# The prompt trunk's neighbourhood attention: all 32 probability tiles turned through VectorE and DRAM, value strips copied in the second head group only

## The chip, the cores and the metric

The kernel runs on one core of one Trainium2 chip. The metric is the device time of one execution in microseconds (us). Before the change it is 2136.32 us, the median of three runs (2136.04 to 2136.45).

Five engines work side by side, each through its own queue of instructions in order: TensorE (PE, matmuls; its weight loads are listed as PEld), VectorE (DVE), ScalarE (ACT), GpSimd (POOL) and SyncE (SP). SP issues most transfers (DMAs), ACT and POOL some. An instruction that waits holds back all that stands behind it in its queue. A "q" behind an engine's name in the profile (SPq, ACTq) is that queue, where DMAs are issued.

## What is computed

One layer of an encoder over two sequences, `x_sample` (512 tokens) and `x_prompt` (1024 tokens). The part that matters here, shortened:

```python
z = xn @ w_in                       # q,k,v of branch A, q,k,v of branch B, two gates
o_a = _gqa_attention(qa, ka, va)    # full attention, 8 heads of 64
o_b = _neighbourhood_attention(qb, kb, vb, rpb)
merged = sigmoid(ga) * (o_a @ w_proj_a) + sigmoid(gb) * (o_b @ w_proj_b)
h = x + merged @ w_out
y = h + relu(rmsnorm(h) @ w_mlp_up) ** 2 @ w_mlp_down
```

In branch B each block of 128 queries (two rows of 64 tokens) sees a band of rows of keys, masked to a window of 16 columns, with a learned bias: `p = softmax(q k^T * scale + bias)`, then `p v`. `p` has queries on the partitions, while its product with v needs keys there: each probability tile has to be transposed.

## The kernel before

All products of float32 values are made in three matmuls of halves: each operand is split into a high part (a rounded copy, made by ACT) and a low part (the remainder, a subtraction by DVE). Line 212 issues all these matmuls; lines 199 and 206 are ACT's and DVE's halves of the splits of weights. A weight tile so passes from DRAM by SP (`raw_...`, line 245), through ACT (high) and DVE (low), to PE.

The two sequences are worked off in turn: first the sample (`NB == 1`), then the prompt (`NB == 2`, about 440 to 1100 us), then the MLP of both. The change touches the prompt only, "the long branch". Its stages:

1. **Two groups of heads (g = 0, 1), each with projections and attention A.** The projections of q, k and v take x (`xs`) against split weights; `zs` and `zvs` are their results in PSUM, `zvs` that of v of branch B (weights `raw_vs`, split into `wh_vs` and `wl_vs`). v of branch B is stored to DRAM (`vds`) for use by row bands. Rope tables (`rts`, line 708) come by SP. Then attention A: scores and exponentials (`ps`), transposes of the probabilities on PE (line 823) with ACT and DVE splitting them (828, 829), outputs `os` (791, 792), `ot_As` and `os_As`, stored to DRAM by ACT (`oads`, line 435). Gate matmuls `gpss` are dealt between them as filling work (`fill.pull`), their results stored as `zgs`.
2. **Value strips.** Branch B wants v in four sets of columns. In attention A of both groups, two copies a unit go from DRAM to DRAM (`vsts<-vds`, lines 801 to 811), each with the four heads of its group: 16 copies of 256 KB a group, on SP. A semaphore of eight, shared by SP's and ACT's DMAs in rotation, makes a copy wait for an earlier DMA, among these ACT's stores of attention.
3. **Branch B: 32 units**, eight heads by four query blocks in the order j = 1, 2, 0, 3 (names end in head and j: `_6_2`). A loop over i runs the steps of several units at once: scores of unit i (`s_unit`: `sbs` on PE, `sbss` on DVE, exponential `pbs` on ACT, scaling by POOL), the transposed and split tile of an earlier one (`t_unit`: `bhs`), the product with v of one before that (`v_unit`: `obs` on PE, `ot_Bs` and `os_Bs` behind it). In each round `f` steps of filling work are pulled, at first projections of the next heads (`pqbs`, `pkbs`, weights `w_bqs`, `w_bks`) and the gates, from i = 25 on projection A (`ppas`, one step is three matmuls of 512 columns, results added by DVE to `mAs`).
4. **Projection B (`ppbs`), the output projection,** and later the MLP.

A tile is transposed in one of two ways. The first 24 units (the set `moved`) take the detour: `turn` (line 1094) transposes 32x32 blocks in place on DVE (STREAM_TRANSPOSE) and stores the tile to DRAM (`tbs`, line 1097); `fetch_t` reads it back with the blocks moved (`bhs<-tbs`, line 1104); ACT makes the high part (line 1116, 128x768), DVE the low one (1117); `v_unit` uses six matmuls of 256 columns. The turn comes one round behind the scores, the fetch two, the split three and the output four. The last eight units (heads 6 and 7) are transposed on PE: six matmuls into two PSUM tiles (`ptbs`, line 1126), two ACT copies (1133) and two DVE subtractions (1134) of 128x384, one round behind the scores, and `v_unit` one more behind with four matmuls (two of 512 columns, two of 256).

The order of each engine's instructions is not simply that of the code. A scheduler orders them as the program is built, by its own estimates, except where the code keeps the program's order. PSUM has four buffers for `ppas`, `gpss`, `obs` and `ptbs` together and two for scores.

Of the kernel before, what the change touches and what calls it, by code (L numbers as in the profile page):

```python
# [22 lines left out]
GRID_W = 64  # L23
# [38 lines left out]
def encoder(ctx: ExitStack, tc: tile.TileContext, xs, outs, w):  # L62
# [356 lines left out]
    def run(tr, nxt, first):  # L419
# [109 lines left out]
        for g in range(2):  # L529
# [230 lines left out]
            with phase(f"phA{N}_{g}") as ph:  # L760
                units = [(h, qb) for h in range(4) for qb in range(NB)]
                PP = {}

                def s_tile(u, j):
                    h, qb = u
                    nm = f"{N}_{g}_{h}_{qb}_{j}"
                    q0 = (qb * 4 + j) * P
                    lhs = qT[h % 2][:, h // 2, q0 : q0 + P]
                    s = big(f"s{nm}")[:, :T]
                    for kb in range(NB):  # L770
                        ks = slice(kb * 512, kb * 512 + 512)
                        nc.tensor.matmul(s[:, ks], lhs, kT[:, 0, ks], start=True, stop=False)
                        nc.tensor.matmul(s[:, ks], lhs, kT[:, 1, ks], start=False, stop=True)  # L773
                    nm_ = sml.tile([P, 1], F32, tag="nm", name=f"nm{nm}")
                    nc.vector.tensor_reduce(nm_, s, axis=AX.X, op=ALU.max, negate=True)  # L775
                    p = ph.tile([P, T], F32, tag="P", name=f"p{nm}", bufs=8)
                    l = sml.tile([P, 1], F32, tag="l", name=f"l{nm}")
                    nc.scalar.activation(p, s, AF.Exp, bias=nm_, accum_out=l)  # L778
                    rl = sml.tile([P, 1], F32, tag="rl", name=f"rl{nm}")
                    nc.vector.reciprocal(rl, l)  # L780
                    nc.gpsimd.tensor_scalar(p, p, rl, 1.0, op0=ALU.mult, op1=ALU.mult)  # L781
                    PP[u, j] = p

                o_of = {}

                def pv(u, kc, hi, lo):
                    h, qb = u
                    if kc == 0:
                        o_of[u] = mm(f"o{N}_{g}_{h}_{qb}")
                    o = o_of[u]  # L790
                    nc.tensor.matmul(o, vhl[:, kc, :], hi, start=(kc == 0), stop=False)
                    nc.tensor.matmul(o, vhl[:, kc, :], lo, start=False, stop=(kc == NT - 1))
                    if kc == NT - 1:
                        r0 = (g * 4 + h) * HD
                        finish_o(o, 512, oad[r0 : r0 + HD, qb * 512 : qb * 512 + 512], ph, f"A{N}_{g}_{h}_{qb}")

                for j in range(4):
                    s_tile(units[0], j)
                    fill.pull(2)
                queue = []  # L800
                LAG = 2
                for ui, u in enumerate(units):
                    h, qb = u
                    if NB == 2:
                        hs = slice(4 * g, 4 * g + 4)
                        for a in range(2 * (ui % 2), 2 * (ui % 2) + 2):
                            c0 = (0, 8, 24, 32)[ui // 2]
                            nc.sync.dma_start(
                                vst[ui // 2][:, :, a, hs, :].rearrange("k c h d -> k c (h d)"),
                                vd[:, hs, :].rearrange("(k a c) h d -> a k c (h d)", a=4, c=GRID_W)[a, :, c0 : c0 + 32],  # L810
                            )
                    if first:
                        bias_row(g * 4 + ui)
                        if g == 0 and ui == 1:
                            early["a"] = load_a(1)
                        if g == 0 and ui == 2:
                            early["v"] = load_v(1, slot)
                    nxt_u = units[ui + 1] if ui + 1 < len(units) else None
                    sdone = 0
                    for kc in range(NT):  # L820
                        pt = mm(f"pT{N}_{g}_{h}_{qb}_{kc}")
                        for j in range(4):
                            nc.tensor.transpose(  # L823
                                pt[:, j * P : (j + 1) * P], PP[u, j][:, kc * P : (kc + 1) * P], ident
                            )
                        hi = ph.tile([P, 512], F32R, tag="pth", name=f"pth{N}_{g}_{h}_{qb}_{kc}", bufs=3)
                        lo = ph.tile([P, 512], F32R, tag="ptl", name=f"ptl{N}_{g}_{h}_{qb}_{kc}", bufs=3)
                        nc.scalar.activation(hi, pt, AF.Copy)  # L828
                        nc.vector.tensor_tensor(lo, pt, hi.bitcast(F32), op=ALU.subtract)  # L829
                        queue.append((u, kc, hi, lo))  # L830
                        if nxt_u is not None:
                            while sdone < 4 and kc >= ((0, 1, 3, 4) if NB == 2 else (0, 0, 1, 2))[sdone]:
                                s_tile(nxt_u, sdone)
                                sdone += 1

                        fill.pull(1 if NB == 1 or kc % 4 < 3 else 0)
                        if len(queue) > LAG:
                            pv(*queue.pop(0))
                fill.drain()
                for item in queue:  # L840
                    pv(*item)
# [80 lines left out]
        with phase(f"phB{N}") as ph:  # L922
# [2 lines left out]
            rects, strips, bms, PT = {}, {}, {}, {}  # L925
            units = [(h, j) for h in range(8) for j in (1, 2, 0, 3)]
            n = len(units)
            moved = set(units[: n - 8]) if NB == 2 else set()

            def raw_here(name):  # L930
                if NB == 2:
# [157 lines left out]
            def turn(u):  # L1089

                h, j = u
                pm = PT[u]
                blocks = pm.rearrange("p b f k i -> p (b f k) i")
                tc.keep_in_program_order(nc.vector.transpose(blocks, blocks))
                PT[u] = dram.tile([P, 4, halves * nkc * 32], F32, name=f"tb{N}_{h}_{j}")
                with behind("SP"):
                    nc.sync.dma_start(PT[u], pm.rearrange("p b f k i -> p b (f k i)"))

            def fetch_t(u):

                h, j = u
                hl = ph.tile([P, 2, 4, halves, nkc, 32], F32R, tag="bh", name=f"bh{N}_{h}_{j}", bufs=3)
                with behind("SP"):
                    op = nc.sync.dma_start(
                        hl[:, 1].rearrange("p a f k i -> p a (f k i)").bitcast(F32),
                        PT[u].rearrange("(a i) b w -> (i b) a w", i=32),
                    )
                note("SP", op)
                PT[u] = hl
# [77 lines left out]
            for i, u in enumerate(units):  # L1187
                ls = 3 if u in moved else 3 - NB
                due_t.setdefault(i + ls, []).append(u)
                due_v.setdefault(i + ls + 1, []).append(u)  # L1190
            for i in range(n + 4 - NB):
                if moved:
                    slot_no[0] = i
                if i < n - 8:
                    f = (5 if i < 2 else 2 + i % 2) if NB == 1 else 5 - (i % 6 == 5)
                else:
                    f = 3 + i % 2 if NB == 1 else 8
                if NB == 2 and i == n - 11:
                    pa = proj_a(ph, raw_here)
                    next(pa)  # L1200
                if i < n:
                    late = i > 0 and units[i - 1] in moved
                    if i > 1 and units[i - 2] in moved:
                        fetch_t(units[i - 2])
                    s_unit(units[i], partial(turn, units[i - 1]) if late else None)
                    h, j = units[i]
                    if j == 1 and h < 7:
                        if moved:
                            prep_bias(h + 1)
                        else:  # L1210
                            prep(h + 1)
                    if moved and h > 0:
                        with behind("SP"):
                            prep_v(h, j)
                    if i % 8 == 6 and i + 2 < n:

                        qp = qkproj(i // 8 + 1, wqk, qk)
                        for _ in range(NC8):
                            next(qp)
                    if i % 8 == 7 and qp is not None:  # L1220
                        for _ in qp:
                            pass
                        qp = None
                        if i + 1 < n - 8:
                            wqk = load_qk(i // 8 + 2, held)
                if NB == 2 and i == n - 7:
                    for u in due_v.pop(i):
                        v_unit(u)
                    fill.drain()
                    fill.add(pa)  # L1230
                fill.pull(f // 2)
# [745 lines left out]
```

## Time and profile before

| | |
|---|---|
| median of three runs | 2136.32 us |
| the profiled execution's own time | 2136.87 us |
| its span, first to last instruction | 2135.0 us |
| mean granted clock of PE | 0.997 |
| PE busy | 2099.9 us |
| attention A of group 0, of group 1 | about 452 to 587, 650 to 785 us |
| branch B's units | about 782 to 1059 us |
| projection A in it | 998 to 1059 us |

A row of a stretch ("windows") gives its start and end, its length, then the busy time of PE, PEld, DVE, ACT and POOL with their instructions, the granted clock, the DMA engines' share and GB/s. A row of a timeline gives start, duration, engine, line, operation, out<-in, and in brackets the idle time before it with its releaser. "x6" in it stands for six instructions that follow each other; a duration of one matmul holds some fill time that overlaps with the next, so the step from start to start is the price. A row of waits gives the total, how often, and the longest.

### The profile page before, as it was taken

The page shows a single profiled execution, that of the slowest core. Times are in us where ns is not written, and L with a number is a line of the kernel's source. Part 1 is how long each engine was busy: PE and PEld are TensorE (multiplying, and loading weights), DVE is VectorE, ACT ScalarE, POOL GpSimd, SP SyncE. Part 2 cuts the span into 40 slices and gives each one's busy share as a digit, 9 for nine tenths or more (in the row PEclk, how much of TensorE's full clock was granted, in tenths as well). Part 3 has the DMA queues.
Part 4 walks back from the last instruction along what each step waited for, and adds up shares of the span by engine and source line. Part 5 has one row for each costly group of instructions (what it writes and reads, how often), then busy time and mean ns, then how long its engine had stood idle before and what let it go on. Part 6 is the DMA issues. An engine that isn't in the chain of part 4 may idle for free.

```text
span 2135.0 us, 31762 instructions
## 1 busy us (share of the span) xinstructions
PE 2099.9 (98%) x10871; PEld 1840.2 (86%) x10871; DVE 1483.2 (69%) x2793; ACT 1146.3 (54%) x2487; POOL 362.0 (17%) x446
## 2 busy tenths in 40 slices
PE   9999999999989999999999999999999999999998
PEld 8888778988888888888888899999999988888887
DVE  6665786767647756787882877778777777759563
ACT  6664653767556645555531556556655643434352
POOL 2232310323233314442101200003000000000000
PEclk9999999999999999999999999999999999999999
DMA  6437557520133038876472666578445799688561
GB/s 192 133 99 212 148 165 254 184 89 29 59 111 107 25 97 245 244 219 196 153 246 103 203 196 193 162 249 210 158 146 158 259 351 344 215 276 282 166 203 64
DMA packets 340072, 381.31 MB, mean 179 GB/s; under 512 B 30911, under 2 KB 267079, under 8 KB 339911
## 3 DMA queue, kind: packets, MB, share of 16 engines
q1 hardware_dynamic: 301687, 313.99, 46.9%
q10 hardware_dynamic: 31072, 45.11, 6.0%
q0 software_dynamic: 7152, 20.19, 3.5%
q8 instruction: 86, 1.41, 0.3%
q14 instruction: 75, 0.61, 0.1%
HBM read 282.68 MB, written 105.71 MB: 182 GB/s over the span
## 4 chain that ended last, share of the span: by engine, by line
PE 53%; DVE 1%; issue 0%; ACT 0%; POOLq 0%; POOL 0%; ACTq 0%; DVEq 0%
PE dn L212 20%; PE ua L212 6%; PE ud L212 6%; PE uc L212 6%; PE ops L212 4%; PE ub L212 3%; PE ppbs L212 2%; PE ppas L212 2%; PE dnf L212 2%; PE pt L353 0%; PE obs L212 0%; PE gpss L212 0%; PE sbs L212 0%; PE ptbs L1126 0%; DVE A L1452 0%
## 5 line engine op out<-in xcount | busy, mean ns | idle before, releaser
L212 PE MATMUL dn<-wd,ah 128*128 128x512 f32 x1248 | 384.3, 389 | 0.0
L212 PEld LDWEIGHTS dn<-wd,ah 128*128 128x128 f32 x1248 | 234.2, 188 | 48.7
L212 PE MATMUL dn<-wd,al 128*128 128x512 f32 x624 | 242.8, 389 | 0.0
L1451 ACT ACTIVATE ah<-ar 128x512 fp32r<-128x512 f32 x168 | 104.4, 628 | 206.0 <-PE dn L212 186.7
L212 PE MATMUL gpss<-xs_0h,w_gs 128*128 128x512 f32 x512 | 188.7, 402 | 0.8 <-DVE ot_Bs L472 0.4
L1452 DVE TENSOR_TENSOR al<-ar,ah 128x512 fp32r<-128x512 f32 x168 | 114.4, 687 | 75.5 <-ACT ah L1451 67.9
L212 PE MATMUL ud<-B,A 128*128 128x384 f32 x768 | 143.6, 334 | 0.7 <-DVE c L1569 0.7
L212 PE MATMUL uc<-B,A 128*128 128x384 f32 x768 | 143.7, 334 | 0.0
L212 PE MATMUL ua<-B,A 128*128 128x384 f32 x768 | 138.8, 334 | 0.0
L212 PEld LDWEIGHTS dn<-wd,al 128*128 128x128 f32 x624 | 117.1, 188 | 24.2
L781 POOL TENSOR_SCALAR ps<-ps,rls 128x1024 f32<-128x1024 f32 (+1 forms) x96 | 96.8, 1010 | 226.4 <-DVE rls L780 201.0
L212 PEld LDWEIGHTS ud<-B,A 128*128 128x128 f32 x768 | 133.9, 188 | 1.1 <-DVE c L1569 1.1
L212 PEld LDWEIGHTS uc<-B,A 128*128 128x128 f32 x768 | 134.1, 188 | 0.2 <-ACT A L1451 0.2
L212 PEld LDWEIGHTS ua<-B,A 128*128 128x128 f32 x768 | 133.7, 188 | 0.2
L829 DVE TENSOR_TENSOR ptls<-pTs,pths 128x512 fp32r<-128x512 f32 x160 | 107.7, 686 | 37.3 <-ACT pths L828 36.3
L828 ACT ACTIVATE pths<-pTs 128x512 fp32r<-128x512 f32 x160 | 94.0, 597 | 73.4 <-PE pTs L823 71.3
L212 PE MATMUL ops<-wh_os,mgs 128*128 128x512 f32 x384 | 119.4, 390 | 0.0
L775 DVE TENSOR_REDUCE nms<-ss 128x1 f32<-128x1024 f32 (+1 forms) x96 | 99.9, 1041 | 25.6 <-PE ss L773 25.1
L212 PEld LDWEIGHTS gpss<-xs_0h,w_gs 128*128 128x128 f32 x512 | 96.3, 189 | 18.9 <-DVE w_gs L206 0.7
L778 ACT ACTIVATE ps<-ss,nms 128x1024 f32<-128x1024 f32 (+1 forms) x96 | 93.2, 972 | 23.4 <-DVE nms L775 20.6
L180 POOL TENSOR_TENSOR rs_f<-ms_f,mhalf 128x1 f32<-128x1 f32 x6 | 4.0, 667 | 590.7 <-DVE ms_f L176 590.7
L823 PEld LDWEIGHTS pTs<-ident,ps 128*128 128x128 f32 x640 | 77.7, 140 | 28.6 <-POOL ps L781 4.3
(287 smaller groups left out, 5152.4 us busy)
## 6 DMA issues: line engine op xcount, KB each, us to landing
ar<-ud SPq DMA_DIRECT2D x120, 512.0 KB
br<-in_w_mlp_down_dram SPq DMA_DIRECT2D x72, 512.0 KB
rawu<-in_w_mlp_up_dram SPq DMA_DIRECT2D x64, 512.0 KB
ud<-c ACTq DMA_DIRECT2D x128, 192.0 KB
raw_gs<-in_w_in_dram SPq DMA_DIRECT2D x32, 512.0 KB
ud<-cs SPq DMA_DIRECT2D x64, 192.0 KB
tbs<-pbs SPq DMA_DIRECT2D x24, 384.0 KB
bhs<-tbs SPq DMA_DIRECT2D x24, 384.0 KB
```

What stands on the lines that cost most here:

```text
L180: nc.gpsimd.tensor_tensor(r[:, :n], m[:, :n], mhalf[:, :n], op=ALU.pow)
L212: op = nc.tensor.matmul(out, a, b, **kw)
L775: nc.vector.tensor_reduce(nm_, s, axis=AX.X, op=ALU.max, negate=True)
L778: nc.scalar.activation(p, s, AF.Exp, bias=nm_, accum_out=l)
L781: nc.gpsimd.tensor_scalar(p, p, rl, 1.0, op0=ALU.mult, op1=ALU.mult)
L823: nc.tensor.transpose(pt[:, j * P : (j + 1) * P], PP[u, j][:, kc * P : (kc + 1) * P], ident)
L828: nc.scalar.activation(hi, pt, AF.Copy)
L829: nc.vector.tensor_tensor(lo, pt, hi.bitcast(F32), op=ALU.subtract)
L1451: nc.scalar.activation(hi, src, AF.Copy)
L1452: nc.vector.tensor_tensor(lo, src, hi.bitcast(F32), op=ALU.subtract)
```

## The change

Three edits, all for the prompt:

- The strip copies are made in group 1 only, and each takes all eight heads: 16 copies of 512 KB instead of 32 of 256 KB.
- `moved` holds all 32 units. The last eight take the detour too, with its lags of three and four rounds, so the loop has two rounds more (i to 35). `fetch_t` and the last `turn` get conditions of their own, since there are no more scores beside them, and a `v_unit` that came early at i = 25 is no longer taken out.
- From i = 24 on six steps of filling work are pulled a round instead of eight.

```diff
@@ attention A
-                    if NB == 2:
-                        hs = slice(4 * g, 4 * g + 4)
+                    if NB == 2 and g == 1:
                         for a in range(2 * (ui % 2), 2 * (ui % 2) + 2):
                             c0 = (0, 8, 24, 32)[ui // 2]
                             nc.sync.dma_start(
-                                vst[ui // 2][:, :, a, hs, :].rearrange("k c h d -> k c (h d)"),
-                                vd[:, hs, :].rearrange("(k a c) h d -> a k c (h d)", a=4, c=GRID_W)[a, :, c0 : c0 + 32],
+                                vst[ui // 2][:, :, a].rearrange("k c h d -> k c (h d)"),
+                                vd.rearrange("(k a c) h d -> a k c (h d)", a=4, c=GRID_W)[a, :, c0 : c0 + 32],
                             )
@@ branch B
-            moved = set(units[: n - 8]) if NB == 2 else set()
+            moved = set(units) if NB == 2 else set()
...
-            for i in range(n + 4 - NB):
+            for i in range(n + 3 if NB == 1 else n + 4):
...
-                    f = 3 + i % 2 if NB == 1 else 8
+                    f = 3 + i % 2 if NB == 1 else 6
...
+                if 1 < i < n + 2 and units[i - 2] in moved:
+                    fetch_t(units[i - 2])
+                if i == n and moved:
+                    turn(units[i - 1])
                 if i < n:
                     late = i > 0 and units[i - 1] in moved
-                    if i > 1 and units[i - 2] in moved:
-                        fetch_t(units[i - 2])
                     s_unit(units[i], partial(turn, units[i - 1]) if late else None)
...
                 if NB == 2 and i == n - 7:
-                    for u in due_v.pop(i):
-                        v_unit(u)
                     fill.drain()
```

How the order moves is seen in three places. Lines behind the first edit are one lower in the kernel after.

First, SP at the end of group 0 and the start of group 1 (`rawkvs` and `raw_vs` are weights of the k and v projections, `rts` rope tables). Before:

```order
L510 DMA rawkvs_1_7022<-in_w_in_dram 128x8x64 x2
L808 DMA vsts_0_4661<-vds_4660 128x1x512 x4
L808 DMA vsts_1_4662<-vds_4660 128x1x512 x4
L808 DMA vsts_2_4663<-vds_4660 128x1x512 x4
L808 DMA vsts_3_4664<-vds_4660 128x1x512 x4
L245 DMA raw_vs_1_0_7031<-in_w_in_dram 128x4x256
L245 DMA raw_vs_1_4_7038<-in_w_in_dram 128x4x256
L708 DMA rts_1_0_7047<-in_rope_dram 128x128
```

After:

```order
L510 DMA rawkvs_1_7006<-in_w_in_dram 128x8x64 x2
L245 DMA raw_vs_1_0_7015<-in_w_in_dram 128x4x256
L245 DMA raw_vs_1_4_7022<-in_w_in_dram 128x4x256
L245 DMA raw_gs_2304_4_0_7603<-in_w_in_dram 128x8x128
L708 DMA rts_1_0_7031<-in_rope_dram 128x128
```

The sixteen copies of group 0 are gone from between the weights of k and those of v.

Second, ACT at the end of attention A and the start of branch B (`qBs` and `kBs` are the first heads' q and k out of `pqbs` and `pkbs`). Before:

```order
L435 DMA zgs_0_4665<-sgs_2304_7_1_9215 128x512
L475 ACTIVATE ot_As_1_3_1_9222<-os_1_3_1_9142 64x512
L435 DMA oads_4667<-os_As_1_3_1_9224 64x512
L992 ACTIVATE qBs_0_9258<-pqbs_0_0_9261 64x4x128 x2
L1013 ACTIVATE kBs_0_0_9259<-pkbs_0_0_9296 64x512 x2
```

After:

```order
L435 DMA zgs_0_4665<-sgs_2304_7_1_9199 128x512
L475 ACTIVATE ot_As_1_3_1_9206<-os_1_3_1_9126 64x512
L435 DMA oads_4667<-os_As_1_3_1_9208 64x512
L199 ACTIVATE w_bqs_0_9226<-raw_bqs_0_0_9224 128x1024
L199 ACTIVATE w_bks_0_9232<-raw_bks_0_0_9230 128x1024
L199 ACTIVATE w_gs_3328_0_9238<-raw_gs_3328_0_0_9236 128x1024
L991 ACTIVATE qBs_0_9242<-pqbs_0_0_9245 64x4x128 x2
```

Before, the split of `w_bqs_0` stands some 115 rows earlier, among attention's exponentials; after, three splits stand behind attention's last store and ahead of `qBs`.

Third, PE in projection A. Before, from one output to the next:

```order
L212 MATMUL obs_6_2_11752<-bhs_6_2_11608,vss_6_11406 128x512 x2
L212 MATMUL obs_6_2_11752<-bhs_6_2_11608,vss_6_11406 128x2x128 x2
L212 MATMUL sbs_7_1_11765<-kBs_3_1_11132,qBs_3_11130 128x384 x4
L212 MATMUL ppas_3_0_11799<-oXs_0_0_11033,w_pas_3_11691 128x512 x3
L212 MATMUL ppas_3_0_11799<-oXs_0_1_11036,w_pas_3_11691 128x512 x3
L212 MATMUL ppas_3_0_11799<-oXs_0_2_11037,w_pas_3_11691 128x512 x3
L212 MATMUL ppas_3_0_11799<-oXs_0_3_11038,w_pas_3_11691 128x512 x3
L1126 MATMUL ptbs_6_3_0_11815<-ident,pbs_6_3_11677 128x128 x3
L1126 MATMUL ptbs_6_3_1_11816<-ident,pbs_6_3_11677 128x128 x3
L212 MATMUL ppas_3_1_11828<-oXs_0_0_11033,w_pas_3_11691 128x512 x3
```

(three more steps of `ppas` follow.) After:

```order
L212 MATMUL obs_6_2_11812<-bhs_6_2_11599,vss_6_11390 128x2x128 x6
L212 MATMUL sbs_7_0_11828<-kBs_3_1_11116,qBs_3_11114 128x384 x4
L212 MATMUL ppas_3_1_11803<-oXs_0_2_11021,w_pas_3_11651 128x512 x3
L212 MATMUL ppas_3_1_11803<-oXs_0_3_11022,w_pas_3_11651 128x512 x3
L212 MATMUL ppas_4_0_11872<-oXs_0_0_11017,w_pas_4_11781 128x512 x3
L212 MATMUL ppas_4_0_11872<-oXs_0_1_11020,w_pas_4_11781 128x512 x3
L212 MATMUL ppas_4_0_11872<-oXs_0_2_11021,w_pas_4_11781 128x512 x3
L212 MATMUL ppas_4_0_11872<-oXs_0_3_11022,w_pas_4_11781 128x512 x3
L212 MATMUL obs_6_0_11890<-bhs_6_0_11677,vss_6_11390 128x2x128 x6
```

The transposes `ptbs` are gone, an output is six matmuls, a round has six steps of `ppas`, and the outputs come two rounds later against the scores.

## The prediction

> **What bounds the kernel now.** I read the page's busy line first, then the waits of TensorE (PE) alone over the prompt trunk (440 to 1070 us), since only that trunk is touched.
>
> ```profile
> PE 2099.9 (98%) x10871; PEld 1840.2 (86%) x10871; DVE 1483.2 (69%) x2793; ACT 1146.3 (54%) x2487; POOL 362.0 (17%) x446
> PE zvs L212 <- ACT wh_vs L199: 5.7, 1, 5.7
> PE sbs L212 <- DVE kBs L1015: 2.3, 2, 1.8
> PE obs L212 <- DVE bhs L1117: 1.4, 2, 1.0
> ```
>
> PE has work for 98% of the span; its listed waits (total, times, longest) in the trunk come to about 11 us, over half of them one wait. So an edit can gain in two ways only: take PE work away, or take that wait away. It loses where it makes PE wait anew. The third view is the table of stages (PE, PEld, DVE, ACT, POOL busy, then granted clock, DMA share, GB/s):
>
> ```profile
> 599.40:605.30 5.90, 5.43 (x22) 4.92 (x23) 5.38 (x8) 1.80 (x5) 2.96 (x4) 0.51 0.23 65
> 985.00:998.00 13.00, 11.16 (x52) 9.51 (x51) 11.81 (x26) 8.38 (x17) 5.26 (x8) 0.87 0.81 237
> 998.00:1059.00 61.00, 60.90 (x309) 51.56 (x308) 49.35 (x118) 36.17 (x72) 17.54 (x22) 1.00 0.55 167
> 925.11:953.67 28.56, 28.56 (x148) 24.99 (x147) 25.07 (x60) 18.55 (x38) 16.30 (x17) 1.00 0.84 246
> ```
>
> The first row is the stretch behind the long wait: half the clock. The third, "the tail", holds projection A and the last units: PE full, VectorE (DVE) 81% busy. The fourth is a run of units on the detour: PE full with DVE at 25.07 of 28.56, 88%.
>
> **Part 1: start of group 1 (copies gone from group 0).** SP's timeline, its queue engine, shows why PE waited:
>
> ```profile
> 583.19 3.69 SPq L808 DMA_DIRECT2D vsts<-vds  x4
> 586.99 4.00 SPq L245 DMA_DIRECT2D raw_vs<-in_w_in_dram  x2
> 598.32 1.06 ACT L199 ACTIVATE wh_vs<-raw_vs 128x1024 fp32r<-128x1024 f32 x1 [3.29 <-DMA raw_vs<-in_w_in_dram]
> 599.43 0.58 PE L212 MATMUL zvs<-wh_vs,xs_0h 128*128 128x256 f32 x1 [5.74 <-ACT wh_vs L199]
> 605.68 0.38 PE L622 MATMUL pqs<-ident,rrs 128*128 128x128 f32 x2
> 610.14 0.28 PE L212 MATMUL zvs<-wh_vs,xs_0h 128*128 128x256 f32 x1
> 611.93 0.28 PE L212 MATMUL zvs<-wh_vs,xs_0h 128*128 128x256 f32 x1
> ```
>
> The load of v's weights stands on SP behind sixteen strip copies, which group 0 hands out until 586.9; weights, ScalarE's (ACT) split and PE then follow in a chain. The change leaves group 0 no copies, and the load follows the kv weights. It then waits only for buffers used early in the group. Both splits are ready before PE comes (it ran out of work at 599.43 − 5.74 = 593.7). This removes the 5.74 us. It removes the slow stretch too: 24 zvs matmuls and one of zs took from 599.43 to 605.68, 6.25 us; at full rate 15 steps take 611.93 − 610.14 = 1.79, 0.12 each, so 25 take 3.1. Sum 5.74 + 3.15 = **−8.9**. Late next are the rope tables (loaded behind v's weights before, moved with them) and the next q transposes; they are used after zvs. Bounds: −5.7 (the clock falls for another reason) and −9.2. If another wait takes half its place, −4.
>
> **Part 2: start of phase B (splits moved behind attention's end).** By the order, the splits of the first w_bqs, w_bks and w_gs no longer stand among ACT's exponentials but behind the last output of attention A; PE's order has not moved. In the trace of before:
>
> ```profile
> 782.06 0.39 PE L212 MATMUL pqbs<-xs_0h,w_bqs 128*128 128x512 f32 x1
> 782.98 0.68 DVE L484 TENSOR_TENSOR os_As<-os,ot_As 64x512 f32<-64x512 f32 x1 [2.15 <-ACT ot_As L475]
> 783.69 0.46 ACTq L435 DMA_DIRECT2D oads<-os_As  x1
> L206 DVE TENSOR_TENSOR w_bqs<-raw_bqs,w_bqs x16: 650/676/761, 157.4 to 930.4; 128x512 fp32r<-128x512 f32 x16
> L199 ACT ACTIVATE w_bqs<-raw_bqs x8: 1045/1048/1067, 156.3 to 925.7; 128x1024 fp32r<-128x1024 f32 x8
> ```
>
> PE begins pqbs at 782.06, straight after attention. Afterwards it needs the split, and ACT issues attention's last store ahead of it, which waits for DVE until 783.69. ACT is free at 784.15, and 1.05 of split ends at 785.2: a new wait of 3.15 us. The third matmul needs the low half from DVE, 0.65 later, where two matmuls cover 0.45: 0.2 more. The price of the clock comes from the nearest rows:
>
> ```profile
> 987.41 1.28 PE L212 MATMUL sbs<-kBs,qBs 128*128 128x384 f32 x3 [1.84 <-DVE kBs L1015]
> 988.50 0.63 PE L212 MATMUL gpss<-xs_0h,w_gs 128*128 128x512 f32 x1
> 988.92 0.63 PE L212 MATMUL gpss<-xs_0l,w_gs 128*128 128x512 f32 x1
> 991.23 0.40 PE L212 MATMUL gpss<-xs_1l,w_gs 128*128 128x512 f32 x1
> 991.46 0.62 PE L212 MATMUL gpss<-xs_1h,w_gs 128*128 128x512 f32 x2
> ```
>
> After a wait of only 1.84 us the 512-wide steps are 0.42 instead of 0.23, up to 991; 3.5 us at half rate lose about 1.7. The 5.74 us wait lost 2.7 (3.15 less the 0.4 or so that PE waited for the low half). For 3.15 I take 2.2, between the two. Sum 3.15 + 0.2 + 2.2 = **+5.5**, bounds +3.2 and +6.5. The Trainium skill ("TensorE: Matmul & The Clock Gate", Part 1: The HAM clock gate) says that the clock halves after at least one idle window of some 3.4 us. By that rule a wait of 3.15 costs no clock, and this part is +3.4; the 1.84 us wait above, half rate behind it, disagrees.
>
> Some of group 1's copies, now of 512 KB, wait on SP for attention's last stores (783.69) and for one another, with phase B's first loads behind them. The first PE work that needs these is the first unit's output:
>
> ```profile
> 827.95 0.99 PE L212 MATMUL obs<-bhs,vss 128*128 128x256 f32 x6 [0.45 <-DVE bhs L1117]
> ```
>
> That is 44 us later; before, the last copy was out at 792 and the output waited 0.45. Nothing, unless the queue is held past 810. The same output's first store of the detour also moves behind a bias load on SP, by some 1 us, which lengthens this wait by no more than that; I count nothing.
>
> **Part 3: the tail.** Each of the last eight units loses six PE transposes, its output goes in 6 narrow matmuls instead of 4, and DVE exchanges two subtractions from PSUM for one turn and one wider subtraction:
>
> ```profile
> 1054.22 0.82 PE L1126 MATMUL ptbs<-ident,pbs 128*128 128x128 f32 x6
> 1054.79 2.99 PE L212 MATMUL ppas<-oXs,w_pas 128*128 128x512 f32 x12
> 1050.78 0.85 PE L212 MATMUL obs<-bhs,vss 128*128 128x512 f32 x4
> 1051.46 2.91 PE L212 MATMUL ppas<-oXs,w_pas 128*128 128x512 f32 x12
> 948.82 0.89 PE L212 MATMUL obs<-bhs,vss 128*128 128x256 f32 x6
> 949.54 0.87 PE L212 MATMUL sbs<-kBs,qBs 128*128 128x384 f32 x4
> L1134 DVE TENSOR_TENSOR bhs<-ptbs,bhs 128x384 fp32r<-128x384 f32 x16 | 8.2, 545 | 0.2 <-ACT bhs L1133 0.2
> L1117 DVE TENSOR_TENSOR bhs<-bhs 128x768 fp32r<-128x768 f32 x6 | 5.7, 954 | 3.8 <-ACT bhs L1116 3.8
> L1094 DVE STREAM_TRANSPOSE pbs<-pbs 128x768 f32<-128x768 f32 x4 | 3.9, 968 | 0.0
> ```
>
> By starts, the transposes take 0.57 a unit and the output 0.72 instead of 0.68: 8 × (−0.57 + 0.04) = −4.2 for PE, so 56.8 of the tail's 61. ACT has one copy for two and is under 60% busy. DVE gets 8 × (0.97 + 0.95) − 8.2 = +7.2: 56.6 us of work. So in the tail DVE is as full as PE. Six fill steps a unit make the period 18 × 0.23 + 0.72 + 0.71 = 5.6 us on PE, while DVE's list for one unit sums to about 6.2; the last four units without scores give some back. PE may run ahead by the four PSUM buffers that projection, outputs and (before) transposes share, and DVE's list must be done near the end, since the last output needs its subtraction. At the 88% of the run above, 56.6 us of DVE take 64.3 (+3.3); at 95% they take 59.6; at 100% PE's own −4.2 stands. The highest share of this tail is near the middle value:
>
> ```profile
> 1043.88:1051.46 7.58, 7.58 (x40) 6.44 (x39) 7.20 (x18) 5.09 (x10) 1.46 (x2) 1.00 0.44 137
> ```
>
> 7.20 of 7.58 is 95%, with PE unhindered. I take 59.6, that is **−1.4**, bounds −4.2 and +3.3. Latency of the detour: turn to ACT's copy, shortest kind and longest,
>
> ```profile
> 929.36 0.97 DVE L1094 STREAM_TRANSPOSE pbs<-pbs 128x768 f32<-128x768 f32 x1
> 937.98 0.85 ACT L1116 ACTIVATE bhs<-bhs 128x768 fp32r<-128x768 f32 x1 [0.21 <-DMA bhs<-tbs]
> 841.32 0.98 DVE L1094 STREAM_TRANSPOSE pbs<-pbs 128x768 f32<-128x768 f32 x1 [1.16 <-POOL pbs L1085]
> 855.29 0.85 ACT L1116 ACTIVATE bhs<-bhs 128x768 fp32r<-128x768 f32 x1 [1.77 <-DMA bhs<-tbs]
> ```
>
> 8.6 and 14.0 us. The unit's output comes three periods behind its turn, 16.7 us, so PE does not wait for the transfers themselves. What is queued behind the subtraction on DVE is a rival. The last output's way to the next projection is as long as before, under that projection's first nine matmuls.
>
> Sum: −8.9 + 5.5 − 1.4 = **−4.8**. The profiled execution took 2136.87 (span 2135.0 and 1.87 around it), 0.55 above the median of the three runs, 2136.32; it would take 2132.1, and the median 2131.5.
>
> **The rivals.**
>
> *The tail stays PE-bound*: DVE's waits for PE fill up with the new work, PE keeps its whole −4.2: 2128.7. For it speaks PE's full share at 88% DVE; against it a list longer than PE's period.
>
> *No clock price at phase B's start*: the new wait is too short to halve the rate: −8.9 + 3.4 − 1.4, 2129.4. This is the outcome by the skill's rule just named. The row at 987.41 speaks against it.
>
> *The first stall changes hands*: v's weights come early, but rope or a split on the busy DVE (5.38 of 5.90 there) is late, and half the gain stays: −4 + 5.5 − 1.4, 2136.4. That the change does not do what it says is this same case.
>
> *Slower: DVE stops behind the detour.* By the order, a unit's subtraction in the tail stands right behind the turn of the next unit, ahead of its successors' scores; in the earlier run it stood behind the turn of the second next. A late transfer then stops DVE. Two periods are at least (turn to subtraction) + (about 3 us of DVE from the subtraction to the turn after). With 8.6 + 0.85 that makes 6.2 a period, no more than DVE's own list. It decides from about 12 to ACT's copy: (12.85 + 3) / 2 = 7.9 a period, seven of them 55.5 from the first of these turns (taken at the tail's start, 998), and 14.5 more through the last subtraction and output, so the tail ends at 1068 instead of 1059: +9, and −8.9 + 5.5 + 9 gives 2141.9. For it: 14.0 us was seen. Against: there transfers came every 4.85 us on one queue, here they are further apart.
>
> **How the numbers follow.** Forecast 0.40 (own range 2129 to 2134.5); PE-bound tail 0.17; no clock price 0.13; stall changes hands 0.20; DVE stops 0.10. About 0.2%, 4.3 us, is what a measurement of this kernel can tell from no change. The forecast lies just beyond that bound at 2132.0: 0.24 of its 0.40 count as faster, with nearly all of the next two (0.28) 0.52; slower is the last rival, 0.10; the rest, 0.38, is the same. The range takes the low bounds of parts 1 to 3 nearly whole (−9.2 + 3.2 − 4.2 = −10.2) and at the top the stall changing hands with DVE at 88% (−4 + 5.5 + 3.3 = +4.8, cut to +2.7): 2126.3 to 2139.0.
>
> **What would show it.** Right: no wait of zvs for wh_vs, zvs at 0.12 steps; a wait of pqbs of about 3 us for w_bqs with the clock at half behind it; no ptbs in the trunk, and from the first ppas to the first ppbs some 59 us with DVE above 90%. Wrong: PE waiting for the subtraction or for mAs in the tail by more than 3 us together, DVE idle there for bhs, or a new wait within 20 us behind the start of group 1.

## The result, and the profile after

| | before | after |
|---|---|---|
| median | 2136.18 us (4 runs, 2135.86 to 2136.45) | 2169.51 us (4 runs, 2165.52 to 2170.81) |
| ratio | | 1.0153, 95% interval [1.0135, 1.0171] |
| the profiled execution's span | 2135.0 us | 2163.5 us |
| mean granted clock | 0.997 | 0.989 |

The change makes the kernel 1.5% slower, far outside the forecast's range. The profiled execution of after took 2165.52 us, the lowest of its runs; between the two profiles the span grows by 28.5 us, and it is these that the text explains. The other three executions took 2169.42 to 2170.81; what makes their 4 to 5 us more is not shown by any trace. The busy line of the page first:

```profile
PE 2095.9 (97%) x10839; PEld 1836.7 (85%) x10839; DVE 1486.0 (69%) x2793; ACT 1142.2 (53%) x2479; POOL 365.3 (17%) x446
```

PE has 4.0 us less to do than before (2099.9), as the transposes are gone, and the span is longer: so PE waits more. The waits of PE in the prompt trunk (total, times, longest):

```profile
PE sbs L212 <- ACT kBs L1012: 33.8, 1, 33.8
PE pqbs L212 <- ACT w_bqs L199: 3.1, 1, 3.1
PE sbs L212 <- DVE kBs L1014: 2.6, 2, 1.8
PE ppbs L212 <- ACT oXs L480: 2.0, 1, 2.0
```

The 5.7 us wait for v's weights is gone, the foretold wait of `pqbs` is there, and one wait that was not foretold decides everything: 33.8 us of one `sbs` for `kBs`, the scores of a unit for ACT's part of k. Its cause lies in the timelines of ACT and of POOL (start, duration, then in brackets the idle time before and its releaser):

```profile
790.84 0.59 ACT L1012 ACTIVATE kBs<-pkbs 64x512 fp32r<-64x512 f32 x1 [1.45 <-DVE kBs L1014]
826.88 1.06 ACT L199 ACTIVATE w_gs<-raw_gs 128x1024 fp32r<-128x1024 f32 x1 [35.45 <-DMA raw_gs<-in_w_in_dram]
...
830.82 0.59 ACT L991 ACTIVATE qBs<-pqbs 64x512 fp32r<-64x512 f32 x1
...
833.68 1.19 ACT L1012 ACTIVATE kBs<-pkbs 64x512 fp32r<-64x512 f32 x2
```

```profile
821.98 3.51 POOL L1032 TENSOR_TENSOR bms<-rects,msks 128x384 f32<-128x384 f32 x4 [49.92 <-DMA rects<-biases]
825.44 0.64 POOL L1018 DMA_DIRECT2D kBs<-kBs  x1
```

```profile
834.92 0.69 PE L212 MATMUL sbs<-kBs,qBs 128*128 128x384 f32 x1 [33.85 <-ACT kBs L1012]
```

ACT stands still for 35.45 us, POOL for 49.92, each in front of an instruction that waits for a load: ACT for gate weights (`raw_gs`), POOL for a bias (`rects`). Behind these two stand the rest of `qBs` and `kBs` and POOL's copy of `kBs`, which need neither load. PE runs out of other work at 801, and its row names ACT's `kBs`; no wait of PE in the trunk is put down to POOL.

In before the order was another: there the same splits of `w_gs` stand behind the last `kBs`, at 812.65 and 818.38. The first of them in before's timeline of ACT:

```profile
806.66 0.59 ACT L1013 ACTIVATE kBs<-pkbs 64x512 fp32r<-64x512 f32 x1 [1.45 <-DVE kBs L1015]
...
812.65 1.05 ACT L199 ACTIVATE w_gs<-raw_gs 128x1024 fp32r<-128x1024 f32 x1
```

So two things meet in after: the loads come late, and the scheduler has put the splits that need them ahead of the `qBs` and `kBs`. The table of stages shows the engines in that stretch, and then the tail and the start of projection B (PE, PEld, DVE, ACT, POOL, granted clock, DMA share, GB/s):

```profile
775.00:785.00 10.00, 8.29 (x35) 6.59 (x36) 4.72 (x12) 4.14 (x5) 0.00 (x0) 1.00 0.48 114
795.00:805.00 10.00, 6.08 (x27) 4.69 (x25) 0.00 (x0) 0.00 (x0) 0.00 (x0) 1.00 0.26 105
800.90:835.00 34.10, 0.25 (x2) 0.08 (x1) 4.47 (x13) 4.58 (x7) 4.10 (x5) 0.57 0.68 198
1027.00:1084.00 57.00, 56.73 (x286) 48.69 (x285) 52.93 (x118) 31.52 (x64) 16.92 (x21) 1.00 0.83 266
1084.00:1100.00 16.00, 13.69 (x52) 10.30 (x51) 13.17 (x27) 6.14 (x11) 0.00 (x0) 0.89 0.77 246
```

Why the loads are late stands in SP's timeline and in SP's waits, in after and then in before:

```profile
746.82 56.04 SPq L807 DMA_DIRECT2D vsts<-vds  x12
802.97 4.68 SPq L941 DMA_DIRECT2D rects<-biases  x1
807.70 13.67 SPq L949 DMA_DIRECT2D vss<-vsts  x4
821.46 0.49 SPq L245 DMA_DIRECT2D raw_gs<-in_w_in_dram  x1
```

```profile
SPq L807 <- DMA oads<-os_As: 100.9, 4, 46.2
SPq L807 <- DMA zgs<-sgs: 31.4, 3, 16.0
```

```profile
SPq L808 <- DMA zgs<-sgs: 112.2, 5, 59.1
...
SPq L808 <- DMA oads<-os_As: 14.2, 2, 9.3
```

The first copies go out at 645, but SP then waits 132 us for ACT's stores of attention and of the gates, which share the semaphores of the copies. Twelve of the sixteen copies are issued only from 746.8 on. They leave SP at 803, the strip loads at 821, and only then the gate weights. The waiting itself is not new: in before SP waits 126 us for these stores in group 1. What is new is that twice the bytes come behind it.

The copies themselves are slow. From 795 to 805 they have the DMA engines nearly to themselves, and these are busy to 0.26 and move 105 GB/s; at that rate a copy of 512 KB takes 5 us. A copy's outer dimension counts four groups of rows. The Trainium skill ("DMA: Bandwidth & Descriptors", Rules for kernel authors) says that an outermost dimension of fewer than 16 entries confines a transfer to at most that many DMA engines. By that rule it is four of 16, a share of 0.25; the trace agrees with 0.26.

### The profile page after: what moved, and what is told of

Read it like the earlier page. It is cut to its first block, busy times and chain, and to the rows that moved or that the text cites. A ratio compares the mean times of both kernels' runs of the same rounds, so it can differ in the third digit from the quotient of the medians.

```text
span 2163.5 us, 31685 instructions
## 1 busy us (share of the span) xinstructions
PE 2095.9 (97%) x10839; PEld 1836.7 (85%) x10839; DVE 1486.0 (69%) x2793; ACT 1142.2 (53%) x2479; POOL 365.3 (17%) x446
## 4 chain that ended last, share of the span: by engine, by line
PE 50%; DVE 2%; DMA 1%; issue 1%; ACT 0%; POOLq 0%; POOL 0%; DVEq 0%; ACTq 0%; SPq 0%
PE dn L212 19%; PE ua L212 6%; PE ud L212 6%; PE uc L212 6%; PE ops L212 4%; PE ub L212 3%; PE ppbs L212 2%; PE dnf L212 2%; DMA bhs<-tbs 1%; PE pt L353 0%; PE ppas L212 0%; PE gpss L212 0%; DMA tbs<-pbs 0%; DVE ot_Bs L472 0%; DVE oXs L206 0%
```

## The experiments

Nothing is left out of the computation in any of them. All times are medians; ratios are to the kernel before on the same chip.

| kernel | us | ratio, 95% interval |
|---|---|---|
| copies in both groups (edits 2 and 3 alone) | 2138.62 | 1.0008 [0.9999, 1.0017] |
| copies in the second group only (edit 1 alone) | 2166.15 | 1.0137 [1.0120, 1.0154] |
| copies on 16 engines | 2128.12 | 0.9956 [0.9942, 0.9971] |
| copies on POOL's queue | 2150.04 | 1.0062 [1.0047, 1.0077] |
| wide copies, released late | 2135.72 | 0.9991 [0.9982, 1.0001] |
| projection B's splits on POOL, wide copies | 2127.66 | 0.9956 [0.9944, 0.9969] |
| edit 1 alone with wide copies | 2127.82 | 0.9957 [0.9944, 0.9969] |
| wide copies, eight steps a round | 2132.51 | 0.9977 [0.9968, 0.9986] |
| wide copies, four steps in the last rounds | 2128.41 | 0.9960 [0.9947, 0.9972] |
| wide copies, five steps a round | 2126.41 | 0.9953 [0.9939, 0.9967] |

Theory, from the two traces: **the backlog**. Copies late and narrow keep SP until 821, and ACT and POOL stop in front of the loads behind them. Rival: **the detour**, more transfers and a fuller VectorE, delays branch B.

**1. Copies in both groups.** From after, edit 1 is undone:

```diff
-                    if NB == 2 and g == 1:
+                    if NB == 2:
+                        hs = slice(4 * g, 4 * g + 4)
...
-                                vst[ui // 2][:, :, a].rearrange("k c h d -> k c (h d)"),
+                                vst[ui // 2][:, :, a, hs, :].rearrange("k c h d -> k c (h d)"),
```

> Edit 1 undone, the rest as in the kernel after: strip copies of 256 KB in both groups, all 32 units on the detour, six fill steps. Theory, the backlog (the loss comes from sixteen 512 KB copies in one group, which keep SP and with it the first loads of branch B until 821 us): no wait of sbs near 800, the wait of zvs (5.7 us) is back, no wait of pqbs; the tail gains 4.4 us and loses 4.3 at the start of projection B, as in the kernel after, so 2134 to 2138 us, no change against before. Rival, the detour (the loss comes from the eight more detours, their 6 MB of transfers and DVE's work): 2155 us or more, whatever the copies do.

Measured 2138.62, no different from before within the interval, though 0.6 above the expected range. PE's waits:

```profile
PE zvs L212 <- ACT wh_vs L199: 5.6, 1, 5.6
...
PE ppbs L212 <- ACT oXs L480: 2.0, 1, 2.0
PE ppas L212 <- DVE ot_Bs L472: 1.4, 1, 1.4
```

The first wait of before is back, both waits at the start of branch B are gone, and those of `ppbs` stay. So these last belong to the detour, and the detour and its six steps are worth nothing in sum, as far as an interval of some 2 us either way can tell.

**2. Copies in the second group only.** From before, edit 1 alone is made:

```diff
-                    if NB == 2:
-                        hs = slice(4 * g, 4 * g + 4)
+                    if NB == 2 and g == 1:
...
-                                vst[ui // 2][:, :, a, hs, :].rearrange("k c h d -> k c (h d)"),
+                                vst[ui // 2][:, :, a].rearrange("k c h d -> k c (h d)"),
```

> Edit 1 alone on the kernel before: sixteen copies of 512 KB in group 1, 24 units on the detour, eight fill steps. Theory, the backlog: the 33.8 us wait of the first sbs is there, the zvs wait is gone (-9), pqbs waits 3 us; 2162 to 2171 us, within 3 us of the kernel after. Rival, the detour: -9 and +5.5 alone, about 2132 us.

Measured 2166.15, with 24 units on the detour.

```profile
PE sbs L212 <- ACT kBs L1012: 30.4, 1, 30.4
PE pqbs L212 <- ACT w_bqs L199: 3.1, 1, 3.1
```

This is 3.4 below after, with overlapping intervals. Edit 1 alone brings the long wait. The rival falls.

**3. Copies on 16 engines.** From after, the copies' dimensions change places, so that 32 columns stand outermost instead of four groups of rows. Bytes and places are the same:

```diff
-                                vst[ui // 2][:, :, a].rearrange("k c h d -> k c (h d)"),
-                                vd.rearrange("(k a c) h d -> a k c (h d)", a=4, c=GRID_W)[a, :, c0 : c0 + 32],
+                                vst[ui // 2][:, :, a].rearrange("k c h d -> c k (h d)"),
+                                vd.rearrange("(k a c) h d -> a c k (h d)", a=4, c=GRID_W)[a, c0 : c0 + 32],
```

> The kernel after with one thing changed: each copy names its 32 columns as the outer dimension and its four row groups as the inner one, so that 32 instead of 4 outer entries are there to be dealt to the DMA engines; bytes, count, place in the code and queue are the same. Theory, the backlog with its cause in the shape (the copies ran with a DMA share of 0.25, a quarter of the engines): the share rises towards 1 while copies run, the last ones land within a few us of their issue, the first sbs waits under 8 us; 2126 to 2136 us. Rival, the release (copies are late because each waits on SP for a store of attention by ACT, and 512 KB or its shape play no part): the wait stays over 20 us and the time over 2155 us.

Measured 2128.12, 0.44% below before. SP's timeline and waits:

```profile
645.70 62.97 SPq L807 DMA_DIRECT2D vsts<-vds  x16
```

```profile
SPq L807 <- DMA oads<-os_As: 23.2, 2, 17.1
SPq L807 <- DMA zgs<-sgs: 21.1, 1, 21.1
```

The sixteen copies are out by 708.7 instead of 803, and SP waits 44 us for ACT's stores instead of 132. On ACT the two splits of `w_gs` still stand ahead of the `qBs`, as in after, at 788.09, but their loads are issued from 748.8 on and nothing stops. So it is the lateness of the loads that makes the stall. Two things have changed with one edit, though: the copies are faster, and they are also issued earlier, with shorter waits for the stores. The fifth experiment tries to part them.

**4. Copies on POOL's queue.** From after:

```diff
-                            nc.sync.dma_start(
+                            nc.gpsimd.dma_start(
                                 vst[ui // 2][:, :, a].rearrange("k c h d -> k c (h d)"),
```

> The kernel after with the sixteen copies issued by POOL instead of SP, shape as in the kernel after. Theory, the backlog: the copies no longer stand between attention and branch B on SP, they do not wait for ACT's stores, and at about 5 us each they are through before attention of group 1 ends; no 33.8 us wait, 2126 to 2138 us. Against it, if the DMA engines and not SP's queue were what the first loads waited for, the wait stays above 15 us; and if POOL's issues hold back its scaling of attention's probabilities, PE waits in attention (transposes for ps) by some us.

Measured 2150.04, where 2138 at most was expected. Neither the 33.8 us wait nor that of `pqbs` is left. But attention stops many times over:

```profile
PE ss L772 <- ACT ps L778: 9.3, 11, 2.7
PE os L791 <- ACT pths L827: 2.8, 4, 1.0
...
PE os L792 <- DVE ptls L828: 2.0, 5, 1.1
```

That SP is free removes the stall, as the theory says, and here too the splits of `w_gs` stand ahead of the `qBs` (811.67). The copies have the shape of after's, so the narrow shape alone, without the late release on SP, does not make the stall. Why attention is slower is not shown: the expectation was that POOL's issues hold back its scaling, but POOL's waits for the values it scales by (`rls`) are in total no longer than in experiment 3, 78.9 against 83.7 us, and PE's waits above name ACT and DVE.

**5. Wide copies, released late.** The wide copies of experiment 3 are all issued by the last two units, and a small copy of an attention tile (`vsts<-pths`), overwritten at once, holds each eight back until that tile is there. From after:

```diff
-                    if NB == 2 and g == 1:
-                        for a in range(2 * (ui % 2), 2 * (ui % 2) + 2):
+                    if NB == 2 and g == 1 and ui >= 6:
+                        for y in range(2 * (ui - 6), 2 * (ui - 6) + 2):
+                            nc.sync.dma_start(vst[y][0, 0, :, 0, 0:1]..., mark[-1]...)
+                            for a in range(4):
...
+                        mark.append(hi)
```

> Copies with 32 outer entries as in e3, but held back to where the kernel after has them: four tiny stores of a value of attention's units 6 and 7 into the strips' buffers (the copies then write over it) make eight copies wait for unit 6 and eight for attention's last store, about 775 us; the order of ACT and SP at the start of branch B is that of the kernel after. If the shape is the cause (a quarter of the DMA engines, 5 us a copy), the copies land within about 10 us of their release, the first sbs waits under 8 us, 2127 to 2140 us. If late release alone is the cause, sbs waits over 20 us and the time is over 2150 us.

Measured 2135.72. SP's timeline, and the stages at the start of branch B:

```profile
778.83 6.19 SPq L810 DMA_DIRECT2D vsts<-vds  x8
...
796.13 0.46 SPq L245 DMA_DIRECT2D raw_gs<-in_w_in_dram  x1
```

```profile
778.00:782.00 4.00, 4.00 (x11) 3.25 (x10) 2.92 (x5) 1.08 (x2) 0.00 (x0) 0.50 0.53 141
782.00:786.00 4.00, 4.00 (x16) 3.26 (x16) 0.00 (x0) 0.22 (x1) 0.00 (x0) 0.85 1.01 357
```

Half the copies leave no earlier than 778.8 (after's last was issued at 798), yet they use all DMA engines (1.01, 357 GB/s), the gate weights follow at 796 instead of 821, and `sbs` waits no longer than 1.8 us. So with a late release the wide shape clears SP's queue 25 us earlier than the narrow one. That the stall is absent does not follow from this alone, because ACT's order is not that of after, against what the expectation says. The splits of `w_gs` stand behind the last `kBs` again, as in before:

```profile
804.75 0.60 ACT L1016 ACTIVATE kBs<-pkbs 64x512 fp32r<-64x512 f32 x1 [1.45 <-DVE kBs L1018]
...
810.72 1.05 ACT L199 ACTIVATE w_gs<-raw_gs 128x1024 fp32r<-128x1024 f32 x1
```

What PE would wait with after's order and loads from 796, no run shows, nor how much of the 33.8 us the order makes. Late release, with the order that came with it, costs the rest, 2135.72 against 2128.12: the 3.1 us wait of `pqbs` is back, with half the clock behind it, and `obs` waits 1.6. (The two kernels ran on different chips; their ratios to before, 0.9991 and 0.9956, have separate intervals.)

**6. Projection B's splits on POOL.** What became of the 4.2 us that PE no longer spends on transposes? In after the first outputs of projection B wait (`ppbs <- oXs`). From experiment 3, the low halves of projection B's inputs (`oXs` from `rawos`) go from DVE to POOL:

```diff
-                cut = partial(split, t[:, 0, :], t[:, 1, :])
+                cut = partial(split, t[:, 0, :], t[:, 1, :], eng=nc.gpsimd if br == 1 and NB == 2 else None)
```

> e3 with one thing moved: the low halves of branch B's loaded outputs (oXs from rawos, three tiles, six subtractions of 0.68 us) are made by POOL, which is idle there, instead of DVE. Theory, DVE's lag (its list in projection A is about as long as PE's and finishes some 3 us behind it, which shows as the wait at the start of projection B): 4 us less for DVE, the waits of ppbs (2.0 and 1.1 us) fall under 0.7 together, 2122 to 2126 us. Rival, the chain of the last two outputs itself (ACT, DVE, ACT, DVE in a row) is what is late: the waits stay, 2127 to 2130 us.

Measured 2127.66, a miss: no gain over 2128.12. The wait for the last output's `oXs` fell from 2.0 to 0.7 us, but one for POOL's own part came. Together they are 2.0 us, where the theory had under 0.7 and the rival 3.1:

```profile
PE ppbs L213 <- POOL oXs L206: 1.3, 1, 1.3
...
PE ppbs L213 <- ACT oXs L481: 0.7, 1, 0.7
```

**7. Edit 1 alone with wide copies.** From before, with 24 units on the detour and eight steps:

```diff
-                    if NB == 2:
+                    if NB == 2 and g == 1:
...
-                                vst[ui // 2][:, :, a, hs, :].rearrange("k c h d -> k c (h d)"),
+                                vst[ui // 2][:, :, a].rearrange("k c h d -> c k (h d)"),
```

> The kernel before with e3's copies alone: sixteen wide copies of 512 KB in group 1, the last eight units on PE's transposes, eight fill steps. Theory: the copies are worth -9, and the detour's edits nothing (the 4.4 us that projection A gains are lost at the start of projection B), so 2126 to 2129 us, within 1.5 us of e3. Rival, the detour is worth its 4.4 us: 2131 to 2134 us here. Rival, the detour costs: under 2125 us.

Measured 2127.82, the same as experiment 3 with all 32 (2128.12). The PE waits for `ppbs` are gone. The detour for the last eight units is worth nothing within some 3 us, with narrow copies in both groups (experiment 1) or wide ones in one.

**8. Eight steps a round.** From experiment 3:

```diff
-                    f = 3 + i % 2 if NB == 1 else 6
+                    f = 3 + i % 2 if NB == 1 else 8
```

> e3 with the third edit undone: eight fill steps a round from i = 24 instead of six. Projection A's 64 steps are then through before the last three outputs, and PE waits for the detour of the last units with nothing beside it: 4 to 12 us longer than e3, 2131 to 2140 us. If the six steps were not needed, 2127 to 2130 us.

Measured 2132.51, 4.4 more than with six, as expected: `obs` waits 7.9 us for the detour's subtraction, and `ppbs` not at all. Six steps fit the detour better than eight: experiment 6, with six steps on the same chip, took 2127.66. (The intervals of the ratios with six and eight steps, experiments 3 and 8, just touch.)

**9 and 10. Fewer steps at the end.** Both from experiment 3; steps of projection A that are left over then stand behind the last output:

```diff
-                    f = 3 + i % 2 if NB == 1 else 6
+                    f = 3 + i % 2 if NB == 1 else (6 if i < n else 4)
```

and, in the second, `5` in place of `6`.

> The kernel with copies on 16 engines, but in the last four rounds, which have no scores, four filling steps a round instead of six; the steps of projection A that are left over (about eight, 0.69 us each, 5.5 us) then stand on PE behind the last output and ahead of projection B. Theory that the detour's 4 us are given back only because VectorE is late with the last output (ppbs waits 2.0 and 1.1 us, and the clock behind them): these waits vanish, and the kernel takes 2124 to 2126, 2 to 4 us less than the 2128.1 with six steps. Rival: VectorE is the bound of the whole tail, and then PE only waits elsewhere, for the subtraction of the detour (obs <- bhs) or for a PSUM buffer, by as much: 2127.5 to 2129.

> The same with five filling steps a round from i = 24 to the end; about nine steps are left behind the last output. PE's round is then 5 x 0.69 + 1.43 = 4.9 us instead of 5.6 while VectorE's list for a unit is 6.2 us. Theory that only the end matters: no ppbs wait, 2124 to 2126. Rival, VectorE bounds the tail: the outputs wait for the subtraction (obs <- bhs) by 3 us or more in total, 2128 to 2134, as with eight steps, where these waits were 7.9 us.

Measured 2128.41 and 2126.41. In both the `ppbs` waits vanish, and outputs wait for the detour's subtraction instead. PE's waits from 780 us on with four steps in the last rounds, and, with five throughout, the rows of PE's, DVE's and ACT's timelines at its one long wait:

```profile
PE obs L212 <- DVE bhs L1116: 3.3, 2, 3.0
...
PE obs L212 <- DVE mAs L911: 0.7, 1, 0.7
```

```profile
1027.20 1.62 PE L212 MATMUL obs<-bhs,vss 128*128 128x256 f32 x6 [2.34 <-issue]
```

```profile
1025.79 1.31 DVE L1116 TENSOR_TENSOR bhs<-bhs 128x768 fp32r<-128x768 f32 x1
```

```profile
1022.41 0.85 ACT L1115 ACTIVATE bhs<-bhs 128x768 fp32r<-128x768 f32 x1 [3.62 <-DMA bhs<-tbs]
```

The profile names no releaser for the 2.34 us ("issue"), but the output starts at 1027.20 and DVE's subtraction of `bhs` ends at 1027.10. Ahead of it a transfer of the detour was late: ACT stands 3.62 us in front of its copy of `bhs`, and DVE, 1.51 us idle, waits for what ACT has queued behind. That is the way of the prediction's slower rival, in small, rather than a full VectorE. With four steps the wait moved, as the rival said, and the time stayed. With five the wait is a little under the 3 us that the rival named, and the time fell within the first theory's figures. Yet the 1.7 us to six steps are not resolved, since the intervals overlap. It is the lowest median of all, 10 us below before.

## Why the prediction was wrong, point by point

**Part 1 (−8.9) was right.** PE no longer waits, and from the first `zvs` on each matmul starts 0.12 behind the one before, at full clock. The tile's group before and after with its first and last start:

```profile
L212 PE MATMUL zvs<-wh_vs,xs_0h x32: 278/283/579, 599.4 to 627.4; 128*128 128x256 f32 x32
```

```profile
L212 PE MATMUL zvs<-wh_vs,xs_0h x32: 278/283/283, 593.8 to 618.4; 128*128 128x256 f32 x32
```

627.4 became 618.4: −9.0. The stall did not change hands there; that rival falls.

**Part 2 (+5.5): the wait was right, its clock was not fixed, and the last step failed.** The wait of `pqbs` is 3.1 us, as worked out (3.15). The 2.2 for the clock did not come in this execution, as the rival without a clock price had it: granted 1.00 from 775 to 785. That it stayed away may be chance: behind the same wait the fifth experiment shows 0.50 from 778 to 782, and the second 0.83 in the mean of 770 to 790.

The step that failed is this one: "The first PE work that needs these is the first unit's output", 44 us later, "Nothing, unless the queue is held past 810." SP was held until 821. And the output was the wrong thing to look at. The prediction asked when PE first needs what the held loads bring. It should have asked which instructions of any engine wait for them, and what stands behind those. ACT's split of the gate weights and POOL's bias tile wait for the loads; behind them, in order, stand the remaining `qBs` and `kBs`, for whose scores PE stops at 801. The prediction read that three splits had moved on ACT; it did not follow the order on to the next two, of `w_gs`, which stand behind the last `kBs` in before and ahead of those `qBs` in after. How long SP would be held could have been bounded as well: the copies had doubled in size, and before's trace has a DMA share of 0.32 and 94 GB/s from 785 to 795, while its own copies ended. The step took the end of before's copies (792) and ACT's last store (783.69) as if the copies' own rate did not matter. Its price is 33.85 where 0 stood. That the loads' lateness makes it is shown by experiments 3 and 4, which have these two splits ahead of the `qBs` as well, and no such wait; how the 33.85 divide between late release, narrow copies and the order stays open.

**Part 3 (−1.4) was near in sum by luck, and wrong in its working.** Projection A, with PE's last starts of the tail's tiles, before and after:

```profile
L212 PE MATMUL ppas<-oXs,w_pas x192: 387/389/497, 998.0 to 1057.4; 128*128 128x512 f32 x192
L212 PE MATMUL ppbs<-oXs,w_pbs x192: 387/396/501, 1059.0 to 1103.3; 128*128 128x512 f32 x192
```

```profile
L212 PE MATMUL ppas<-oXs,w_pas x192: 387/389/497, 1026.7 to 1082.3; 128*128 128x512 f32 x192
L212 PE MATMUL ppbs<-oXs,w_pbs x192: 387/396/628, 1083.3 to 1131.9; 128*128 128x512 f32 x192
```

From the first `ppas` to the first `ppbs` 61.0 became 56.6: PE kept all of its −4.2, while DVE was busy for 52.93 of 57.00, 93%, which did not slow PE as 59.6 assumed. Then DVE's backlog came due. From the first `ppbs` to the last, 44.3 became 48.6: +4.3. Two errors cancel: a gain larger than forecast, then a loss that was not forecast. The prediction had said that the last output's way to projection B was "under that projection's first nine matmuls"; PE came early and DVE did not:

```profile
1083.27 1.78 PE L212 MATMUL ppbs<-oXs,w_pbs 128*128 128x512 f32 x7
1085.34 1.21 PE L212 MATMUL ppbs<-oXs,w_pbs 128*128 128x512 f32 x4 [0.28 <-DVE oXs L206]
1088.57 3.70 PE L212 MATMUL ppbs<-oXs,w_pbs 128*128 128x512 f32 x9 [2.03 <-ACT oXs L480]
```

2.3 us of waits and a clock of 0.89 over the 16 us from 1084 make up the 4.3, nearly. Experiments 1 and 7 show a net of nothing in two settings. Whether more of it can be had with other fill stays open: experiment 10 points that way, within its error.

**The slower rival** (DVE stops behind the detour) did not happen with six steps. With eight, DVE's subtraction did hold PE for 7.9 us, and with five a late transfer did for 2.3. A slower outcome came by another mechanism, which no rival held.

In sum, from the shifts of PE's events: −9.0 (v's products), +3.1 (`pqbs`), +33.85 (`sbs`), a remainder of +1.4 (the clock behind the stall is 0.90 from 835 to 860), which puts the last `pqbs` of the prompt's first half (`xs_0h`) 29.4 later (960.4 to 989.8); −5.1 up to the last output (1058.9 to 1083.2), +4.3 at projection B; the span is 28.5 longer.

## What to carry to other kernels

When a change makes transfers larger or later, look not only for the first matmul that needs what stands behind them in the queue: follow each held load to the instruction that waits for it on every engine, and on to what that engine has queued behind. Check too whether the scheduler has moved such an instruction ahead of others. Look at the DMA share during the transfer before trusting its size: one at a quarter of the engines can be made four times as wide by putting a longer dimension outermost, and here that edit, with the earlier issue that came with it, turned a loss of 1.5% into a gain of 0.4%. Work moved off a full engine to one that was nearly full came back here as a wait at the next boundary between stages.

## What the runs showed of the hardware

- The same bytes between DRAM and DRAM: with four entries outermost a DMA share of 0.26 and 105 GB/s; with 32 outermost 1.01 and 357 GB/s (experiment 5, 782 to 786, four such copies and one bias load under way).
- A wait of PE of 3.1 us with the same work behind it: granted clock 1.00 afterwards in after, 0.50 for 4 us in the fifth experiment. In the kernel before, half rate followed a wait of 1.84 us. The Trainium skill ("TensorE: Matmul & The Clock Gate", Part 1: The HAM clock gate) says that the watching window runs freely, some 3.4 us long, which would make it a matter of when the wait falls. That the result differs for the same wait agrees; that a wait well under one window can halve the clock does not follow from its rule of at least one idle window.
- Sixteen copies in a queue that waits for the semaphores of another engine's stores were held for 132 us of group 1's attention in after, and 44 us with the wide copies of experiment 3. In before the same wait in group 1 was 126 us.
